# Attention's page stores on ACT's queue, the third group of the next stage in raw tiles, residual rows tied to the splits

## The chip, the cores and the metric

The kernel runs on one core of a Trainium2 chip. The time is device microseconds (us) of one execution, the median of several runs. TensorE is called PE here, VectorE DVE, ScalarE ACT, GpSimd POOL and SyncE SP.

## What is computed

A two-layer encoder trunk on 1024 positions of width 1024 in float32. Each layer is a mixer and a SwiGLU block, each followed by a LayerNorm over the scaled residual. Layer 0's mixer is latent attention with 8 heads beside a 2-D Fourier mix; layer 1's is a spatial gating unit. Cut to what matters here:

```python
def even_mixer(x, ...):
    attn = mla_attention(q_nope, q_rope, k_nope, k_rope, v)      # 8 heads, softmax over 1024 keys
    return jnp.concatenate([attn, fourier_mix(f)], axis=-1) @ w_out

def reference(x, ...):
    for layer in range(DEPTH):                                   # DEPTH = 2, DN_ALPHA = 4 ** 0.25
        y = even_mixer(x, ...) if layer % 2 == 0 else odd_mixer(x, ...)
        x = layer_norm(DN_ALPHA * x + y, mix_ln_g[layer], mix_ln_b[layer])
        x = layer_norm(DN_ALPHA * x + swiglu(x, ...), ffn_ln_g[layer], ffn_ln_b[layer])
    return x
```

## The kernel before

Float32 products are made of three float32r matmuls (`mm3`, L141 to L143): each operand is split into a high part, cast by ACT (L135), and a low part, a subtraction on DVE (L136). In the trace the high part of a left operand is `xoh`, the low part `xol`; a pair is ready when its L136 has run.

The order is: `even_front` (0 to 175 us), `attention` (to 557.5 us), and then four times a long product of a finished matrix with a weight, in `reduce` (L409): `mix` (the attention's and Fourier's pages by `w_out`), `ffn0`, `odd` and `ffn1`; between them stand `ffn` and `spatial`, which make the pages of the next product. A page is a 128x1024 tile of the left matrix in HBM (512 KB).

`reduce` works with seven products instead of eight per 2x2 block, in the order p = 1, 5, 6, 4, 7, 2, 3. For each p it goes over n groups g of page pairs (two pairs each; n is 3 in `mix`, 6 in `ffn0` and `ffn1`, 4 in `odd`), and a full group is 24 matmuls 128x512 in four PSUM banks, one per slot s. The text writes (p, g) for a group. `stream` (L387 to L398) loads the two operands of a group with SP's DMAs (L396), four of 256 KB in a full group, into tiles `rx` (six of them) and splits them. Of p = 1 the first groups are loaded early by `lead`, during the stage before, into the `raw` tiles that weights use. What p = 1 takes is a plain half of a page; p = 5, 6, 7, 3 and 4 also need sums of two pages, `SA` and `SB`, which DVE makes (`page_sums`, L317 to L320) and POOL stores (`job`, L341, from pages loaded back by L335, or `direct`, L348 and L349); `TA` and `TB` are the same for the weights. The last group of a `reduce` is made from the pages that the stage before finishes last: `mixSA_5` and `mixSB_5` (the job `last`, opened at (1, 1), its sums run behind (5, 0)), `ffn0SA_10`, `oddSA_7` and so on.

The residual rows are eight tiles `xt` of 512 KB, four per half. POOL's queue loads them (`residual`, L463): half 0 at (1, 1), half 1 at (5, 0). In all stages but `mix` two DVE passes apply the last LayerNorm's gain and offset (`gained`, L469 and L470), and `add` (L457) adds a finished bank to them. A tile of `xt` has had another use before; its load waits for the stores out of that earlier tile to land.

DVE, ACT, POOL and SP each run their instructions in the order in which the program's scheduler put them; a waiting instruction holds up all that stands behind it on its engine. `behind(mark)` keeps what is built under it behind that instruction in the order, and `self.marks` are SP's last load, the cast and the subtraction of the last `stream`. In attention each half block ends with a copy of 128x256 from PSUM (L1349, ACT) and a store of it into its page (L1351, SP), 32 in all.

## Time and profile before

| | us |
|---|---|
| median of 3 runs | 2541.53 |
| lowest and highest | 2537.37, 2542.77 |
| the profiled execution | 2541.83 |
| its span, first to last instruction | 2540.0 |
| PE busy in it | 2456.4 |
| DVE, ACT, POOL busy | 1808.9, 1111.1, 318.5 |

The mean granted clock of PE was 0.984 of full speed. In the windows below a row gives for a stretch its length, then for each engine its busy time and the number of instructions, the clock that PE was granted, the busy share of the 16 DMA engines (which reads a little over 1 when they are full) and the rate. In a timeline a row is: start, length, engine, line, operation, output tile and inputs, and in brackets the idle time of the engine just before it with what ended that.

### The profile page before, as it was taken

What the parts mean: (1) busy time and instruction counts of PE and PEld (TensorE: products, weight loads), DVE (VectorE), ACT (ScalarE), POOL (GpSimd) and SP (SyncE); (2) the same over time, 40 slices, a digit from 0 to 9 for tenths busy, and PEclk for the clock granted to TensorE, in tenths of its full rate; (3) what the DMA queues carried; (4) which work ended last, traced back from release to release, by engine and by line L of the source; (5) the groups of instructions that cost most, each with busy time, mean ns of one, the idle gap of its engine ahead of it and who ended that gap; (6) DMA issues with size and microseconds to landing.
All of it is one profiled execution on the core that took longest, in us unless ns stands there. A gap on an engine that the chain in (4) does not pass through costs nothing.

```text
span 2540.0 us, 33155 instructions
## 1 busy us (share of the span) xinstructions
PE 2456.4 (97%) x12294; PEld 2073.4 (82%) x12294; DVE 1808.9 (71%) x2537; ACT 1111.1 (44%) x1711; POOL 318.5 (13%) x527
## 2 busy tenths in 40 slices
PE   8989999998999999999999999988989999999997
PEld 6778888887878888887889998877878888887885
DVE  4348878767886776768678776768777676677667
ACT  3235555544553333333456446653463333333331
POOL 1000111010111111110002132430011111111001
PEclk9999999998999999999999999999999999999998
DMA  4122333138334444467654554667624444549553
GB/s 175 43 89 71 130 110 125 57 138 282 138 118 174 169 168 162 168 252 251 226 182 172 202 203 137 195 244 276 224 73 163 177 166 155 177 164 329 190 188 140
DMA packets 164329, 431.95 MB, mean 170 GB/s; under 512 B 20136, under 2 KB 26952, under 8 KB 164168
## 3 DMA queue, kind: packets, MB, share of 16 engines
q1 hardware_dynamic: 108216, 232.11, 27.8%
q0 software_dynamic: 55952, 197.73, 20.9%
q8 instruction: 96, 1.57, 0.2%
q14 instruction: 65, 0.53, 0.1%
HBM read 286.64 MB, written 138.41 MB: 167 GB/s over the span
## 4 chain that ended last, share of the span: by engine, by line
PE 81%; DVE 6%; issue 5%; DMA 4%; ACT 2%; POOL 1%; SPq 1%; DVEq 0%; ACTq 0%; POOLq 0%
PE b L142 18%; PE b L141 18%; PE b L143 18%; PE S L1316 6%; PE b L912 5%; PE mm L141 4%; PE mm L142 4%; PE mm L143 4%; PE mm L1335 2%; DVE xol L136 1%; DMA rx<-h 1%; PE b L848 1%; DMA x<-xs 1%; ACT xoh L135 1%; DVE st L475 1%
## 5 line engine op out<-in xcount | busy, mean ns | idle before, releaser
L135 ACT CAST whi<-raw 128x1024 fp32r<-128x1024 f32 (+3 forms) x277 | 261.2, 951 | 383.4 <-PE b L142 240.2
L135 ACT CAST xoh<-rx 128x1024 fp32r<-128x1024 f32 (+1 forms) x252 | 244.5, 1011 | 413.5 <-PE b L142 308.8
L141 PE MATMUL b<-xoh,whi 128*128 128x512 f32 x1040 | 410.7, 396 | 7.9 <-ACT xoh L135 7.9
L136 DVE TENSOR_TENSOR wlo<-raw,whi 128x1024 fp32r<-128x1024 f32 (+3 forms) x277 | 303.4, 1099 | 159.3 <-ACT whi L135 157.1
L142 PE MATMUL b<-xol,whi 128*128 128x512 f32 x1040 | 406.8, 391 | 0.0
L143 PE MATMUL b<-xoh,wlo 128*128 128x512 f32 x1040 | 406.4, 391 | 0.0
L136 DVE TENSOR_TENSOR xol<-rx,xoh 128x1024 fp32r<-128x1024 f32 (+1 forms) x252 | 287.6, 1168 | 166.0 <-ACT xoh L135 160.3
L142 PE MATMUL b<-xol,xoh 128*128 128x512 f32 x960 | 379.4, 395 | 22.3 <-DVE xol L136 22.3
L141 PE MATMUL b<-xoh 128*128 128x512 f32 x960 | 376.1, 394 | 8.5 <-ACT xoh L135 8.5
L143 PE MATMUL b<-xoh,xol 128*128 128x512 f32 x960 | 377.5, 393 | 0.0
L141 PEld LDWEIGHTS b<-xoh,whi 128*128 128x128 f32 x1040 | 196.6, 189 | 50.3 <-ACT xoh L135 8.8
L142 PEld LDWEIGHTS b<-xol,xoh 128*128 128x128 f32 x960 | 183.1, 191 | 63.3 <-DVE xol L136 25.5
L143 PEld LDWEIGHTS b<-xoh,wlo 128*128 128x128 f32 x1040 | 196.3, 189 | 41.3
L142 PEld LDWEIGHTS b<-xol,whi 128*128 128x128 f32 x1040 | 196.5, 189 | 40.4 <-issue 0.5
L141 PEld LDWEIGHTS b<-xoh 128*128 128x128 f32 x960 | 182.9, 190 | 47.6 <-ACT xoh L135 9.3
L143 PEld LDWEIGHTS b<-xoh,xol 128*128 128x128 f32 x960 | 183.1, 191 | 38.2
L663 ACT COPY y<-b 128x512 f32<-128x512 f32 x200 | 116.6, 585 | 192.7 <-PE b L143 186.1
L141 PE MATMUL b<-xah,whi 128*128 128x512 f32 x416 | 162.5, 391 | 1.3 <-ACT xah L135 1.3
L142 PE MATMUL b<-xal,whi 128*128 128x512 f32 x416 | 162.0, 389 | 0.0
L143 PE MATMUL b<-xah,wlo 128*128 128x512 f32 x416 | 161.9, 389 | 0.0
L131 DVE TENSOR_TENSOR raw<-raw,raw 128x512 f32<-128x512 f32 (+1 forms) x174 | 128.5, 739 | 28.2 <-DMA raw<-w_up 24.7
L708 DVE TENSOR_TENSOR y<-b,y 128x512 f32<-128x512 f32 x84 | 58.0, 690 | 82.9 <-PE b L143 82.6
(378 smaller groups left out, 4590.9 us busy)
## 6 DMA issues: line engine op xcount, KB each, us to landing
raw<-w_gate SPq DMA_DIRECT2D x44, 512.0 KB, 3.6
raw<-w_up SPq DMA_DIRECT2D x44, 512.0 KB
q<-w_down POOLq DMA_DIRECT2D x44, 512.0 KB, 5.3
h<-x POOLq DMA_DIRECT2D x44, 512.0 KB, 3.7
rx<-h SPq DMA_DIRECT2D x60, 256.0 KB, 3.0
rx<-w_down SPq DMA_DIRECT2D x60, 256.0 KB, 4.3
raw<-o_v SPq DMA_DIRECT2D x16, 512.0 KB, 6.1
x<-o_out POOLq DMA_DIRECT2D x16, 512.0 KB, 5.7
```

What stands on the lines that cost most here:

```text
L131: self.nc.vector.tensor_tensor(out, a, b, op=ALU.subtract)
L135: a = self.nc.scalar.copy(hi, src)
L136: return a.ins, self.nc.vector.tensor_tensor(lo, src, hi.bitcast(F32), op=ALU.subtract).ins
L141: mm(ps, lh, rh, start=start, stop=False, skip_group_check=skip)
L142: mm(ps, lh, rl, start=False, stop=False, skip_group_check=skip)
L143: mm(ps, ll, rh, start=False, stop=stop, skip_group_check=skip)
L475: nc.vector.bn_stats(stats[half, s][:, c, :], xt[half, s][:, c * 512:(c + 1) * 512])
L663: nc.scalar.copy(t, ps)
L708: self.last_v = nc.vector.tensor_tensor(sb, ps, sb, op=op).ins
L912: nc.tensor.matmul(ps[:, i * 256:(i + 1) * 256], l[:, b, k, c], r[:, k, :], start=start and k == 0 and i == 0 and m == 0, stop=k == 3 and ...
L1316: nc.tensor.matmul(sc[:, kb, :], l[:, s], r[:, kb * 512:(kb + 1) * 512], start=i == 0, stop=i == 4)
L1335: nc.tensor.transpose(ps[:, k, :], p[:, kt * P:(kt + 1) * P], self.ident)
```

## The change

The 32 page stores are issued by ACT behind the copy that fills the tile, instead of by SP. In `mix` the group (1, 2) is loaded into `raw` tiles instead of `rx`. A residual row's load is preceded by a DVE MEMSET of its first column (32 in all), placed behind the last split; the rows are asked for two at a time: half 0 at (1, 1) and (1, 2), half 1 at (1, n-1) and (5, 0). `gained` is spread one group further (half 0 up to (5, 0), half 1 from (5, 1) on), and the additions of the first product's banks stand at (5, 1) instead of at the end of p = 1.

```diff
         def load(p, g):
             if (p, g) not in ops:
-                ops[p, g] = self.stream(st, p, groups[g], raws, pairs)
+                ops[p, g] = self.stream(st, p, groups[g], self.raw_tile if st is self.stage["mix"] and (p, g) == (1, 2) else raws, pairs)
...
-        def residual(half):
-            for s in range(4):
-                nc.gpsimd.dma_start(xt[half, s], resid[token(half, s)])
+        def residual(half, s):
+
+            with self.behind(self.marks[2]):
+                nc.vector.memset(xt[half, s][:, 0:1], 0.0)
+            nc.gpsimd.dma_start(xt[half, s], resid[token(half, s)])
...
-                    residual(0)
                     last = self.job(st, M - 1, True) if st is self.stage["mix"] else None
-                if p == 5 and g == 0:
-                    residual(1)
+                if p == 1 and 0 < g < 3:
+                    for s in (2 * g - 2, 2 * g - 1):
+                        residual(0, s)
+                if (p == 1 and g == n - 1) or (p == 5 and g == 0):
+                    for s in (0, 1) if p == 1 else (2, 3):
+                        residual(1, s)
...
-                if p in (1, 5) and g > 1:
-                    spread([lambda s=s: gained(p == 5, s) for s in slots], g - 2, n - 2)
+                if p == 1 and g > 1:
+                    spread([lambda s=s: gained(0, s) for s in slots], g - 2, n - 1)
+                if p == 5 and g == 0:
+                    spread([lambda s=s: gained(0, s) for s in slots], n - 2, n - 1)
+                if p == 5 and g > 0:
+                    spread([lambda s=s: gained(1, s) for s in slots], g - 1, n - 1)
+                if (p, g) == (5, 1):
+                    for s in slots:
+                        add(0, s, lo, 1, True)
...
-                        if p == 1:
-                            add(0, s, lo, p, True)
-                        elif p == 5:
+                        if p == 5:
...
-                        else:
+                        elif p == 2:
...
                 nc.scalar.copy(page, ps)
                 o = qb % 2 * 512 + qb // 2 * 256
-                nc.sync.dma_start(mix[hp * 2 + h][:, o:o + 256], page)
+                nc.scalar.dma_start(mix[hp * 2 + h][:, o:o + 256], page)
```

What this does to the order of the engines is shown at three places. Lines behind the residual load stand two lower in the changed kernel (L469 is L471 there), and lines of the later stages ten.

First, POOL and DVE at the start of `mix`. `mix6` and `mix7` are the last two pages, loaded into `raw966` and `raw967`, from which `mixSA_5` and `mixSB_5` are made, the sums that (5, 2) needs; `x`, `q` and `y` are residual rows. POOL before:

```order
L335 DMA raw966_5668<-mix6_83 128x1024
L341 DMA mixSA_4_117<-raw878_5243 128x1024
L341 DMA mixSB_4_123<-raw879_5244 128x1024
...
L463 DMA x956_5622<-x 128x1024
L463 DMA q957_5623<-x 128x1024
L463 DMA q958_5624<-x 128x1024
L463 DMA y959_5625<-x 128x1024
L335 DMA raw967_5669<-mix7_84 128x1024
L463 DMA x952_5618<-x 128x1024
```

POOL with the change:

```order
L341 DMA mixSB_4_123<-raw879_5244 128x1024
L335 DMA raw966_5664<-mix6_83 128x1024
...
L335 DMA raw967_5665<-mix7_84 128x1024
...
L465 DMA x956_5622<-x 128x1024
L465 DMA q957_5623<-x 128x1024
...
L465 DMA x955_5621<-x 128x1024
L341 DMA mixSA_5_118<-raw966_5664 128x1024
L341 DMA mixSB_5_124<-raw967_5665 128x1024
```

The last page is now loaded ahead of all eight residual rows, and the eight stand ahead of the two stores of its sums. On DVE there, `raw964` and `raw965` are group (1, 2), `rx968` and `rx969` (5, 0), `rx974` and `rx975` (5, 1). Before:

```order
L136 TENSOR_TENSOR xol_5607<-rx969_5729,xoh_5606 128x1024
L457 SCALAR_TENSOR_TENSOR x956_5622<-x956_5622,b960_5626 128x512
L317 TENSOR_TENSOR raw967_5669<-raw966_5668,raw967_5669 128x512
L457 SCALAR_TENSOR_TENSOR q957_5623<-q957_5623,b961_5633 128x512
L318 TENSOR_TENSOR raw966_5668<-raw966_5668 128x512
L136 TENSOR_TENSOR xol_5607<-rx974_5772,xoh_5606 128x1024
L457 SCALAR_TENSOR_TENSOR q958_5624<-q958_5624,b962_5640 128x512
L457 SCALAR_TENSOR_TENSOR y959_5625<-y959_5625,b963_5647 128x512
L319 TENSOR_TENSOR raw966_5668<-raw967_5669,raw966_5668 128x512
L136 TENSOR_TENSOR xol_5607<-rx975_5777,xoh_5606 128x1024
L320 TENSOR_TENSOR raw967_5669<-raw967_5669,raw966_5668 128x512
```

With the change:

```order
L136 TENSOR_TENSOR xol_5607<-raw965_5659,xoh_5606 128x1024
L464 MEMSET x956_5622 128x1
...
L136 TENSOR_TENSOR xol_5607<-rx969_5733,xoh_5606 128x1024
L464 MEMSET x954_5620 128x1
L464 MEMSET x955_5621 128x1
L317 TENSOR_TENSOR raw967_5665<-raw966_5664,raw967_5665 128x512
L136 TENSOR_TENSOR xol_5607<-rx974_5776,xoh_5606 128x1024
L318 TENSOR_TENSOR raw966_5664<-raw966_5664 128x512
L136 TENSOR_TENSOR xol_5607<-rx975_5781,xoh_5606 128x1024
L319 TENSOR_TENSOR raw966_5664<-raw967_5665,raw966_5664 128x512
L457 SCALAR_TENSOR_TENSOR x956_5622<-x956_5622,b960_5626 128x512
L320 TENSOR_TENSOR raw967_5665<-raw967_5665,raw966_5664 128x512
```

One addition of p = 1 (L457) stands ahead of L320, where four did; MEMSETs stand ahead of the sums.

Second, DVE in `ffn0`. `rx1544` and `rx1545` are group (1, 4), `rx1546` and `rx1547` (1, 5). Before:

```order
L319 TENSOR_TENSOR x1521_9735<-x1522_9736,x1488_9550 128x512
L469 TENSOR_TENSOR q1531_9756<-q1531_9756,gb1540_9785 128x1024
L320 TENSOR_TENSOR x1522_9736<-x1520_9715,x1521_9735 128x512
L470 TENSOR_TENSOR q1531_9756<-q1531_9756,gb1541_9787 128x1024
L469 TENSOR_TENSOR x1530_9755<-x1530_9755,gb1540_9785 128x1024
L136 TENSOR_TENSOR xol_5607<-rx1544_9879,xoh_5606 128x1024
L470 TENSOR_TENSOR x1530_9755<-x1530_9755,gb1541_9787 128x1024
L136 TENSOR_TENSOR xol_5607<-rx1545_9884,xoh_5606 128x1024
L469 TENSOR_TENSOR q1532_9757<-q1532_9757,gb1540_9785 128x1024
L136 TENSOR_TENSOR xol_5607<-rx1546_9915,xoh_5606 128x1024
L470 TENSOR_TENSOR q1532_9757<-q1532_9757,gb1541_9787 128x1024
L136 TENSOR_TENSOR xol_5607<-rx1547_9920,xoh_5606 128x1024
```

With the change:

```order
L319 TENSOR_TENSOR x1521_9743<-x1522_9744,x1488_9558 128x512
L464 MEMSET x1530_9763 128x1
L136 TENSOR_TENSOR xol_5607<-rx1544_9889,xoh_5606 128x1024
L320 TENSOR_TENSOR x1522_9744<-x1520_9723,x1521_9743 128x512
L136 TENSOR_TENSOR xol_5607<-rx1545_9894,xoh_5606 128x1024
L471 TENSOR_TENSOR q1531_9764<-q1531_9764,gb1540_9793 128x1024
L472 TENSOR_TENSOR q1531_9764<-q1531_9764,gb1541_9795 128x1024
L136 TENSOR_TENSOR xol_5607<-rx1546_9925,xoh_5606 128x1024
L471 TENSOR_TENSOR x1530_9763<-x1530_9763,gb1540_9793 128x1024
L136 TENSOR_TENSOR xol_5607<-rx1547_9930,xoh_5606 128x1024
L472 TENSOR_TENSOR x1530_9763<-x1530_9763,gb1541_9795 128x1024
```

The pass over `x1530` has moved behind the splits of (1, 4) and stands now between the two of (1, 5). On POOL the load of `x1530` has moved from ahead of the stores of `ffn0SA_10` and `ffn0SB_10` to behind them.

Third, DVE in `odd`. `rx2049` and `rx2050` are group (5, 0), `rx2055` and `rx2056` (5, 1); `x2004` and `x2005` hold the last two pages, whose sums go to `oddSA_7` and `oddSB_7`. Before:

```order
L136 TENSOR_TENSOR xol_5607<-rx2049_15026,xoh_5606 128x1024
L469 TENSOR_TENSOR q2031_14829<-q2031_14829,gb2044_14910 128x1024
L470 TENSOR_TENSOR y2033_14831<-y2033_14831,gb2045_14912 128x1024
L317 TENSOR_TENSOR x2005_14624<-x2004_14623,x2005_14624 128x512
...
L470 TENSOR_TENSOR q2032_14830<-q2032_14830,gb2045_14912 128x1024
L320 TENSOR_TENSOR x2005_14624<-x2005_14624,x2004_14623 128x512
L457 SCALAR_TENSOR_TENSOR x2030_14828<-x2030_14828,b2034_14832 128x512
...
L457 SCALAR_TENSOR_TENSOR y2033_14831<-y2033_14831,b2038_14865 128x512
L136 TENSOR_TENSOR xol_5607<-rx2050_15031,xoh_5606 128x1024
L136 TENSOR_TENSOR xol_5607<-rx2055_15068,xoh_5606 128x1024
L136 TENSOR_TENSOR xol_5607<-rx2056_15073,xoh_5606 128x1024
```

With the change:

```order
L136 TENSOR_TENSOR xol_5607<-rx2049_15042,xoh_5606 128x1024
L136 TENSOR_TENSOR xol_5607<-rx2050_15047,xoh_5606 128x1024
L317 TENSOR_TENSOR x2005_14640<-x2004_14639,x2005_14640 128x512
L471 TENSOR_TENSOR q2031_14845<-q2031_14845,gb2044_14926 128x1024
...
L320 TENSOR_TENSOR x2005_14640<-x2005_14640,x2004_14639 128x512
L472 TENSOR_TENSOR q2032_14846<-q2032_14846,gb2045_14928 128x1024
L471 TENSOR_TENSOR y2033_14847<-y2033_14847,gb2044_14926 128x1024
L464 MEMSET x2028_14842 128x1
L136 TENSOR_TENSOR xol_5607<-rx2055_15088,xoh_5606 128x1024
L472 TENSOR_TENSOR y2033_14847<-y2033_14847,gb2045_14928 128x1024
L464 MEMSET x2029_14843 128x1
L136 TENSOR_TENSOR xol_5607<-rx2056_15093,xoh_5606 128x1024
```

The split of `rx2050` has moved ahead of the page sums; those of (5, 1) stand behind them, with two MEMSETs, which overwrite `x2004` and `x2005` and so wait until the two stores have landed.

## Rows read from the trace of the kernel before

**Rows 1.** The page's first part: busy time, share of the span, instructions

```profile
PE 2456.4 (97%) x12294; PEld 2073.4 (82%) x12294; DVE 1808.9 (71%) x2537; ACT 1111.1 (44%) x1711; POOL 318.5 (13%) x527
```

**Rows 2.** PE's waits: who was waited for, us in total, times, longest

```profile
PE b L142 <- DVE xol L136: 22.3, 8, 6.6
PE b L141 <- ACT xoh L135: 16.4, 4, 5.0
```

**Rows 3.** Windows: length, busy (instructions) of PE, PEld, DVE, ACT, POOL, clock, DMA share, GB/s

```profile
565.00:592.50 27.50, 23.05 (x89) 17.88 (x87) 15.38 (x17) 9.36 (x9) 3.55 (x7) 0.88 0.92 341
592.50:605.00 12.50, 7.54 (x25) 5.72 (x24) 6.41 (x8) 2.94 (x3) 0.00 (x0) 0.73 0.78 254
605.00:670.00 65.00, 65.00 (x289) 53.81 (x288) 55.48 (x76) 28.37 (x29) 5.52 (x7) 1.00 0.66 222
1140.00:1155.00 15.00, 9.33 (x33) 7.18 (x32) 12.24 (x12) 3.06 (x5) 1.59 (x3) 0.77 1.00 376
1690.00:1710.00 20.00, 11.07 (x51) 9.25 (x50) 12.19 (x16) 13.06 (x24) 3.11 (x5) 0.74 1.00 370
1725.00:1740.00 15.00, 8.45 (x31) 6.58 (x30) 13.90 (x17) 2.00 (x2) 2.14 (x4) 0.77 0.72 266
2320.00:2335.00 15.00, 9.82 (x34) 7.60 (x33) 11.63 (x11) 2.80 (x4) 1.59 (x3) 0.77 1.01 395
```

**Rows 4.** PE's timeline where mix goes on after its second stop

```profile
597.85 0.80 PE L141 MATMUL b<-xoh 128*128 128x512 f32 x1 [4.96 <-ACT xoh L135]
```

**Rows 5.** SP's timeline at the start of mix

```profile
558.54 0.88 SPq L396 DMA_DIRECT2D rx<-mix  x2
...
593.77 0.32 SPq L396 DMA_DIRECT2D rx<-mixSB  x1
```

**Rows 6.** ACT's timeline there

```profile
570.98 1.04 ACT L135 CAST xoh<-rx 128x1024 fp32r<-128x1024 f32 x1 [2.06 <-DMA rx<-w_out]
...
578.32 2.21 ACT L135 CAST xoh<-rx 128x1024 fp32r<-128x1024 f32 x2 [2.53 <-DMA rx<-mixTA]
...
596.75 2.94 ACT L135 CAST xoh<-rx 128x1024 fp32r<-128x1024 f32 x3 [8.47 <-DMA rx<-mixSB]
```

**Rows 7.** DVE's timeline there

```profile
587.01 0.69 DVE L320 TENSOR_TENSOR raw<-raw,raw 128x512 f32<-128x512 f32 x1
```

**Rows 8.** POOL's timeline there

```profile
587.99 0.54 POOL L341 DMA_DIRECT2D mixSB<-raw  x1 [1.19 <-DVE raw L320]
```

**Rows 9.** All page stores of attention (L1351): nanoseconds min/median/max

```profile
L1351 SPq DMA_DIRECT2D mix<-page x32: 319/325/430, 208.6 to 558.1; - x32
```

**Rows 10.** DVE's groups by line: the shortest operation on one column

```profile
L205 DVE TENSOR_SCALAR rs<-mv 128x1 f32<-128x1 f32 x32 | 4.7, 148 | 0.2
```

**Rows 11.** DVE's timeline in ffn0

```profile
1142.76 1.23 DVE L469 TENSOR_TENSOR x<-x,gb 128x1024 f32<-128x1024 f32 x1 [4.64 <-DMA x<-xs]
```

**Rows 12.** PE's timeline where ffn0 goes on

```profile
1147.44 0.79 PE L142 MATMUL b<-xol,xoh 128*128 128x512 f32 x1 [5.67 <-DVE xol L136]
```

**Rows 13.** POOL's timeline in ffn0

```profile
1132.68 0.53 POOL L463 DMA_DIRECT2D x<-xs  x1
...
1137.28 0.54 POOL L349 DMA_DIRECT2D ffn0SB<-x  x1 [1.65 <-DVE x L320]
...
1146.41 0.53 POOL L463 DMA_DIRECT2D x<-xs  x1 [0.75 <-DMA ffn0SB<-x]
```

**Rows 14.** DVE's timeline in odd

```profile
1726.10 0.69 DVE L317 TENSOR_TENSOR x<-x,x 128x512 f32<-128x512 f32 x1 [1.93 <-DMA tp<-x]
...
1734.30 5.77 DVE L136 TENSOR_TENSOR xol<-rx,xoh 128x1024 fp32r<-128x1024 f32 x5
```

**Rows 15.** PE's timeline where odd goes on

```profile
1735.58 0.79 PE L142 MATMUL b<-xol,xoh 128*128 128x512 f32 x1 [6.55 <-DVE xol L136]
```

**Rows 16.** POOL's timeline in odd

```profile
1730.56 0.54 POOL L861 DMA_DIRECT2D oddSA<-x  x1 [9.05 <-DVE x L319]
...
1733.70 0.53 POOL L463 DMA_DIRECT2D x<-xs  x1 [0.87 <-DMA oddSA<-x]
```

## Prediction

> **What bounds the kernel now.** I read the page's busy times first: PE is busy for 2456.4 us, 97% of the span [rows 1], so only the time in which it stops, or runs slowly after a stop, can be won; about 84 us. Then PE's waits: 22.3 us for low parts of the left operand of the long products and 16.4 us for high parts [rows 2], which is more than any other pair of lines has. Then the windows, since the sum doesn't tell where. In an undisturbed stretch, 605 to 670, a matmul takes 65/289 = 0.225 us [rows 3], so a group of 24 takes 5.4 us. What a stretch loses is its length less its matmuls by 0.225:
>
> - `mix`: 27.5 - 89 x 0.225 = 7.5 to 592.5 us, and 12.5 - 25 x 0.225 = 6.9 from there to 605; 14.4.
> - `ffn0`: 15 - 33 x 0.225 = 7.6.
> - `odd`: 20 - 51 x 0.225 = 8.5 at 1690 (the shapes are mixed there, so this is rough), and 15 - 31 x 0.225 = 8.0 at 1725.
> - `ffn1`: 15 - 34 x 0.225 = 7.4.
>
> These 46 us, all at the starts of the four `reduce`, are 1.8% of the time. Last I read the timelines there, for what ended each stop. In `mix` the second operand of (1, 2) is cast at 570.98 and a later one waits for `rx<-mixSB` until 596.75 [rows 6]. In `ffn0` DVE's L469 waits 4.64 us for a residual row [rows 11], and the splits of (1, 4) stand behind it. In `odd` the split of (5, 0)'s second operand stands behind gains, page sums and additions until 1734.30 [rows 14]. After a stop the granted clock falls (means of 0.73 to 0.88 in these stretches, 1.00 from 605 on [rows 3]), and matmuls run slower until it is back. `mix` loses 6.9 around a stop of 4.96 [rows 3, 4] and `ffn0` 7.6 around one of 5.67 [rows 3, 12], so a stop of 5 us costs 1.9 us more than itself. I take these 1.9 for every stop that is left.
>
> **Page stores to ACT.** 32 issues at 0.325 us [rows 9] come to 10.4 us of ACT's queue, each behind a copy. ACT is busy for 44% of the span [rows 1] and PE sets the pace of attention, so I cost this at nothing. If ACT's slack were gone the price would be all 10.4 us, which I leave to a rival. SP no longer holds the loads of (1, 2) behind the last store; before, they went out at 558.54 [rows 5].
>
> **`mix`, group (1, 2) in raw tiles.** Its loads can run during attention, into tiles that are free then. Nothing remains of the first stop, 7.5 us, and PE would want (5, 2) at 597.85 - 4.96 - 7.5 = 585.4 [rows 3, 4]. So the question is when (5, 2) is ready, and that hangs on L320. Before, L320 started at 587.01 [rows 7], its store went out at 587.99 [rows 8], the reload at 593.77 [rows 5], the cast began at 596.75 [rows 6] and PE at 597.85: 10.8 us. L320 now stands behind the splits of (5, 0) and (5, 1) and one addition of p = 1. Early end: only the end of p = 1 holds it, at 585.4 - 2 x 5.4 = 574.6, then one addition (0.6): L320 at 575.2, (5, 2) at 586.0. Late end: (5, 1) takes the place in SP's queue that (5, 0) had, whose second operand was cast at 578.32 [rows 6]; cast 1.1, split 1.15 (5.77/5 [rows 14]), L319 and the addition 0.6 each give L320 at 581.8 and (5, 2) at 592.6. I take 589.5, about the middle, since 1 MB less is queued ahead of the loads after 558. PE then stops for 4.1, with 1.9 for the slow restart: 6.0 of 14.4 are still lost, a **gain of 8.4** (5.3 to 13). The two stores of the sums now stand behind all eight residual loads, 4 MB, on POOL; that is the weak point of this term.
>
> The store is the longest piece of this chain: 5.8 us from 587.99 to 593.77 for 512 KB [rows 5, 8]. By the Trainium skill, "DMA: Bandwidth & Descriptors", section "Anatomy of one DMA", a transfer from POOL's queue takes 2.0 us plus its bytes at 436 GB/s, an estimate of 3.2 us here, and (5, 2) would come 2.6 us sooner. The row disagrees, with the DMA engines 0.78 to 0.92 busy [rows 3], and the sum goes by the row.
>
> **`ffn0` and `ffn1`.** The pass over `x1530` no longer stands ahead of (1, 4), so PE doesn't stop at 1147.44 - 5.67 = 1141.8 [rows 12] but wants (1, 5) 5.4 us later, at 1147.2. That pass now stands between the two splits of (1, 5), and its row is loaded behind the store of `ffn0SB_10`. This store was issued at 1137.28 and had landed at 1146.41, when POOL let the next load go [rows 13]. I let the row land then too: the pass 1.15, the split 1.15, (1, 5) at 1148.7, a stop of 1.5 and 1.9 for the restart, and 4.2 of 7.6 are gained. Bounds: the row took 10.1 us before (1132.68 to 1142.76 [rows 11, 13]); issued at 1137.8 it would land at 1147.9, and 2.7 are gained; landing three us sooner, all 7.6. I take **4** each for `ffn0` and `ffn1`, whose window reads alike [rows 3].
>
> **`odd`.** (5, 0) is ready in time: PE doesn't stop at 1735.58 - 6.55 = 1729.0 [rows 15] and runs to 1734.4. But (5, 1) now stands behind L317, which waits for a page's store until 1726.10 [rows 14], three more page sums (0.6 each) and five gains (1.15 each), until 1734.3. The MEMSET of `x2028` asks that `oddSA_7` has landed, 3.1 us after its issue (1730.56 to 1733.70 [rows 16]), which is done by then. One split, one gain and the other split bring (5, 1) to 1737.7. A stop of 3.3 and 1.9 leave 2.8 of 8.0, and some of it goes again at (5, 2), behind the four additions. I take **2** (-1 to 6). The stop at 1692 waits for other loads, and I leave its 8.5 as they are; one residual row less beside them could give back 1.4 (512 KB at 370 GB/s [rows 3]), which is in the range only.
>
> **MEMSETs.** 32 operations on one column; the trace has none, the nearest is 148 ns [rows 10], so 4.7 us of DVE in all, 1.2 per stage, beside PE. Up to 0.6 each, as a page sum takes, they would add 4 us of DVE work to a stage, of which the part ahead of a late split counts: 8 MEMSETs by 0.45, at most 3.6 a stage.
>
> **The sum.** 8.4 + 4 + 2 + 4 = 18.4, so the profiled execution's 2541.8 becomes 2523.4. It is 0.3 above the median of the runs shown: **2523 us**. A measurement of this kernel can tell about 0.2% from no change, 5.1 us.
>
> **Rivals.**
>
> *All four stops go* (0.12). The row lands early in `ffn0` and `ffn1`, L320 runs at the end of p = 1, and `odd` finds DVE free: 14.4 + 7.6 + 8.0 + 7.4 = 37, or 2504 us. For it: DVE is idle for some of the stretch in `ffn0` (12.2 of 15 us busy). Against it: in `odd` it is busy for 13.9 of 15 [rows 3].
>
> *The traffic decides, not the order* (0.20). The DMA engines are 0.92 to 1.01 busy in four of the six stretches [rows 3]. If a stop ends when the bytes ahead of it are in, whatever queue asked, only the 1 MB that leaves the crowded stretch of `mix` counts, 3.1 us at its 341 GB/s [rows 3], besides 2 in `odd`, where the share was 0.72: 2536.5 us, on the edge of what can be told. This is what the Trainium skill, "DMA: Bandwidth & Descriptors", section "Issuing engines are not separate DMA queues", would have: transfers from SP, ACT and POOL end up on the same 16 engines and interleave, and moving them between queues saves issue time only. The windows agree that these are full there; they don't show that each stop waited for the total.
>
> *A residual row becomes the stop* (0.06), slower. On DVE the pass over a row blocks the split behind it. If `x1530`, asked for 5 us later, landed 16 us after its issue instead of 10, (1, 5) would be ready at 1156.1: a stop of 8.9 plus 1.9, 3.2 more than the 7.6 of now, in `ffn0` and in `ffn1`. In `mix` the stores of the sums behind 4 MB of rows would be as late and take its gain. That is 2548 us. It decides once a row takes over 13 us. For it: the engines are full until 1155. Against it: 10.1 was the longest before.
>
> *The raw tiles come free late, or ACT loses time* (0.04). The loads of (1, 2) then wait for stores out of these tiles and land near the time of before, or PE waits for ACT in attention. The gain of `mix` is gone: 2532 us.
>
> **How the numbers follow.** The forecast has 0.58. The first two rivals hold the ends: the range is 2508 to 2537, short of the first one's 2504 and up to the second's 2536.5. Faster by over 0.2%, below 2536.4, are the forecast, the first and the last rival and half of the second, 0.84; within 0.2% the other half, 0.10; slower 0.06.
>
> **What would show it.** In the profile after, the stop near 568 must be gone, and a cast of a `raw` tile for (1, 2) must stand before 557; L320 should start between 575 and 582 after which PE stops for 1 to 7 us. L471 must no longer stand ahead of (1, 4), and PE's stops in `ffn0` and `ffn1` should fall from over 5 us to under 3. In `odd` the stop should sit before (5, 1) instead of (5, 0). PE busy should change little and attention keep its length. The prediction is wrong if a stop of 5 us is still there in `ffn0`, if MEMSETs or L471 show waits of more than 4 us ahead of a split, or if `mix` waits for its sums as late as 597.

## The result and the profile after

The changed kernel takes 2524.18 us against 2539.69 for the kernel before in the same runs, a ratio of 0.9935 (95% interval 0.9918 to 0.9952): 0.65% faster. The prediction was 2523.0. In a second set of runs it took 2522.22 against 2538.94, 0.9934 (0.9920 to 0.9947). The first profile of the changed kernel was of a disturbed execution, so all rows of it here are from the second set, called e_again below.

The page's first part, with the columns of [rows 1]; the span is 2519.2 us where it was 2540.0:

```profile
PE 2451.5 (97%) x12294; PEld 2069.8 (82%) x12294; DVE 1809.1 (72%) x2569; ACT 1112.0 (44%) x1711; POOL 318.9 (13%) x527
```

The work is the same, but for 32 more instructions on DVE. PE is busy for 4.9 us less with the same matmuls, and its mean granted clock is 0.989 where it was 0.984; the other 15.9 of the 20.8 us are idle time, most of them in PE's waits (who was waited for, total, times, longest; [rows 2] has those of before):

```profile
PE b L141 <- ACT xoh L135: 14.8, 3, 6.9
PE b L142 <- DVE xol L136: 14.6, 8, 4.2
...
PE b L858 <- ACT whi L849: 5.0, 1, 5.0
```

22.3 us of waits for low parts have become 14.6, and 16.4 for high parts 14.8. The third row is the first stop of `odd`; before, it was 8.93 us.

PE's timeline of the changed kernel at the five places where the long products stop:

```profile
589.67 0.80 PE L141 MATMUL b<-xoh 128*128 128x512 f32 x1 [6.90 <-ACT xoh L135]
...
1140.29 0.50 PE L142 MATMUL b<-xol,xoh 128*128 128x512 f32 x1 [1.92 <-DVE xol L136]
...
1720.09 0.50 PE L142 MATMUL b<-xol,xoh 128*128 128x512 f32 x1 [3.51 <-DVE xol L136]
...
1743.16 0.79 PE L142 MATMUL b<-xol,xoh 128*128 128x512 f32 x1 [4.16 <-DVE xol L136]
...
2315.64 0.50 PE L142 MATMUL b<-xol,xoh 128*128 128x512 f32 x1 [0.77 <-DVE xol L136]
```

In `mix` only the stop before (5, 2) is left [rows 4], at 6.90 us longer than the 4.96 of before, but PE is through it 8.2 us earlier (589.67, not 597.85); 2.3 of these this execution had won before `mix` begins. In `ffn0` 5.67 [rows 12] has become 1.92. In `ffn1` 0.77 is left, and 0.86 at 2324.96, where before had

```profile
2328.05 0.79 PE L142 MATMUL b<-xol,xoh 128*128 128x512 f32 x1 [5.18 <-DVE xol L136]
```

In `odd` 6.55 [rows 15] has become 3.51, one group later, and there is a new stop of 4.16 just ahead of p = 6.

The windows (columns as in [rows 3]) show the same for whole stretches:

```profile
565.00:592.50 27.50, 20.60 (x86) 16.67 (x85) 13.69 (x16) 6.74 (x7) 3.74 (x7) 0.86 0.92 354
592.50:605.00 12.50, 12.50 (x51) 10.20 (x50) 8.94 (x12) 4.07 (x5) 0.00 (x0) 0.90 0.89 309
...
1730.00:1745.00 15.00, 10.84 (x44) 8.62 (x43) 15.00 (x18) 4.00 (x4) 0.00 (x0) 0.90 0.37 119
```

From 592.5 to 605 PE is never idle (12.5 of 12.5, with 51 matmuls where there were 25). In the last row DVE is: 15.00 of 15.00, which is what the new stop of `odd` waits for.

To compare kernels by stage I matched matmuls of the same number in two traces and took by how many us the later kernel is ahead of before, at the start of each stage and behind its stops: at 565 and 640 us of before's trace for `mix`, 1120 and 1200 for `ffn0`, 1680 and 1800 for `odd`, 2310 and 2400 for `ffn1`. The table has what the lead grew by between the two. Medians and ratios are of the timed runs. The four stages are from one profiled execution each; stretches in which two kernels do the same differ too, all that stands ahead of `mix` by up to 4 us, so a stage is good to 1 or 2 us. What the four columns leave out of a whole span is in such stretches: for the changed kernel 2.3 us ahead of `mix`, 2.3 between the stages and 2.1 behind 2400, of 20.8.

| kernel | median us | ratio to before, 95% | mix | ffn0 | odd | ffn1 |
|---|---|---|---|---|---|---|
| predicted | 2523.0 | | 8.4 | 4 | 2 | 4 |
| e_again, the change | 2522.22 | 0.9934 (0.9920 to 0.9947) | 5.3 | 4.0 | -0.4 | 5.3 |
| e_stores | 2534.43 | 0.9981 (0.9972 to 0.9990) | 5.0 | -0.9 | -0.6 | 0.5 |
| e_mix | 2530.69 | 0.9966 (0.9953 to 0.9979) | 6.2 | 0.2 | 0.1 | 0.8 |
| e_rows | 2525.69 | 0.9950 (0.9937 to 0.9962) | 2.5 | 5.4 | -1.9 | 4.3 |
| e_order | 2531.06 | 0.9967 (0.9956 to 0.9979) | 0.6 | 5.0 | -2.2 | 5.1 |
| e_resid | 2522.60 | 0.9933 (0.9921 to 0.9945) | 3.0 | 6.0 | -0.7 | 6.4 |
| e_noorder | 2518.95 | 0.9926 (0.9914 to 0.9938) | 6.7 | 5.9 | 0.9 | 5.7 |
| e_nomemset | 2527.44 | 0.9954 (0.9942 to 0.9966) | 6.6 | 3.3 | -0.7 | 5.7 |
| e_sums_act | 2519.18 | 0.9927 (0.9914 to 0.9940) | 7.6 | 5.4 | -0.2 | 4.9 |
| e_late | 2521.03 | 0.9931 (0.9919 to 0.9944) | 7.2 | 4.9 | -1.4 | 4.9 |
| e_halves | 2517.57 | 0.9919 (0.9905 to 0.9932) | 6.5 | 6.6 | 2.2 | 6.7 |
| e_best | 2512.81 | 0.9901 (0.9885 to 0.9918) | 7.2 | 6.4 | 3.6 | 6.6 |

### The profile page after: what moved, and what is told of

Its sections match the earlier page's. It is cut to its first block, busy times and chain, and to the rows that moved or that the text cites. A ratio compares the mean times of both kernels' runs of the same rounds, so it can differ in the third digit from the quotient of the medians.

```text
span 2729.4 us, 33158 instructions
## 1 busy us (share of the span) xinstructions
PE 2680.0 (98%) x12294; PEld 2135.9 (78%) x12294; DVE 1818.6 (67%) x2569; ACT 1118.1 (41%) x1711; POOL 316.0 (12%) x527
## 4 chain that ended last, share of the span: by engine, by line
PE 94%; DMA 2%; DVE 2%; issue 1%; ACT 0%; SPq 0%; POOL 0%; DVEq 0%; ACTq 0%; POOLq 0%
PE b L141 22%; PE b L143 22%; PE b L142 22%; PE b L922 6%; PE S L1326 6%; PE mm L141 4%; PE mm L142 4%; PE mm L143 4%; PE mm L1345 2%; PE b L858 1%; DMA mixSB<-raw 0%; PE b L376 0%; DVE xol L136 0%; PE b L364 0%; DMA rx<-o_out 0%
## 5 line engine op out<-in xcount | busy, mean ns | idle before, releaser
L141 PE MATMUL b<-xoh,whi 128*128 128x512 f32 x1040 | 439.0, 422 | 7.9 <-ACT xoh L135 7.7
L143 PE MATMUL b<-xoh,wlo 128*128 128x512 f32 x1040 | 434.4, 418 | 0.0
L142 PE MATMUL b<-xol,whi 128*128 128x512 f32 x1040 | 434.0, 417 | 0.0
L142 PE MATMUL b<-xol,xoh 128*128 128x512 f32 x960 | 401.1, 418 | 4.1 <-DVE xol L136 4.0
L141 PE MATMUL b<-xoh 128*128 128x512 f32 x960 | 399.0, 419 | 4.4 <-ACT xoh L135 4.4
L143 PE MATMUL b<-xoh,xol 128*128 128x512 f32 x960 | 401.5, 418 | 0.0
L141 PE MATMUL b<-xah,whi 128*128 128x512 f32 x416 | 173.7, 419 | 0.0
L143 PE MATMUL b<-xah,wlo 128*128 128x512 f32 x416 | 173.4, 417 | 0.0
L142 PE MATMUL b<-xal,whi 128*128 128x512 f32 x416 | 173.2, 416 | 0.0
```

The source lines that it names most:

```text
L141: mm(ps, lh, rh, start=start, stop=False, skip_group_check=skip)
L142: mm(ps, lh, rl, start=False, stop=False, skip_group_check=skip)
L143: mm(ps, ll, rh, start=False, stop=stop, skip_group_check=skip)
```

## The experiments

The theory to test: four separate edits, each of which shortens the stops of its own stage, so that their gains add. The rival that had most for it: the traffic of the residual rows decides, and any edit that thins it helps.

### Again: the changed kernel itself

No edit.

> The changed kernel once more, for a profile at PE's full clock. By the prediction's sum: about 18 us below the kernel before; in the windows mix loses about 6 us instead of 14.4 (565 to 605), ffn0 and ffn1 about 3.5 instead of 7.5 each, odd's second stretch 6 instead of 8. By the rival that the traffic decides: about 5 us below, with stops of over 5 us still there in ffn0 and ffn1.

Measured: 2522.22 us, 0.9934. The size holds, the parts only in `ffn0` and `ffn1`. By the windows above `mix` still loses 27.5 - 86 x 0.225 = 8.2 and 12.5 - 51 x 0.225 = 1.0, together 9.2 us where 6 was expected, and in `odd` the stops behind 1700 add up to 7.67 us (3.51 and 4.16) where before had one of 6.55.

### Stores: the page stores alone

The kernel before, with one line of the change:

```diff
-                nc.sync.dma_start(mix[hp * 2 + h][:, o:o + 256], page)
+                nc.scalar.dma_start(mix[hp * 2 + h][:, o:o + 256], page)
```

> Only the page stores on ACT. If SP's queue was held by the last page store alone, the loads of (1, 2) go out earlier here as far as their rx tiles are free; by my sum the tiles are not, so no difference (within 2 us) from the kernel before. If ACT's slack in attention were gone: up to 10 us slower.

A miss: 2534.43 us, 4.5 below before where nothing was expected. SP's timeline, before and in this run, gives the reason. Before:

```profile
553.35 5.10 SPq L1351 DMA_DIRECT2D mix<-page  x2
558.54 0.88 SPq L396 DMA_DIRECT2D rx<-mix  x2
559.52 0.90 SPq L396 DMA_DIRECT2D rx<-w_out  x2
```

With the stores on ACT (the loads of `mix` are out since 526):

```profile
556.76 0.81 SPq L396 DMA_DIRECT2D rx<-w_out  x2
557.62 0.93 SPq L396 DMA_DIRECT2D rx<-mixSB  x2
```

Half of (1, 2), its pages of `mix`, had stood behind page stores that it doesn't depend on. Without them it goes out 32 us earlier, still into `rx` tiles, and its other half is cast at 562.28 instead of 570.98 [rows 6]. PE's first stop of before, at (1, 2),

```profile
572.08 0.79 PE L141 MATMUL b<-xoh 128*128 128x512 f32 x1 [3.53 <-ACT xoh L135]
573.34 0.80 PE L142 MATMUL b<-xol,xoh 128*128 128x512 f32 x1 [0.47 <-DVE xol L136]
```

is gone: PE passes the same two matmuls without a wait, at 567.47 and after. What is left ahead of (5, 2) are waits of 0.27 and 0.75 at (5, 1), where before waited 0.46. So the raw tiles are not needed to take this stop away.

### Mix: page stores and raw tiles

The two edits that touch `mix` alone, on the kernel before: the line above and

```diff
-                ops[p, g] = self.stream(st, p, groups[g], raws, pairs)
+                ops[p, g] = self.stream(st, p, groups[g], self.raw_tile if st is self.stage["mix"] and (p, g) == (1, 2) else raws, pairs)
```

> Only the page stores on ACT and the group (1, 2) in raw tiles; residual rows, gains and additions as before. If the first stop of mix is a matter of the loads of (1, 2) alone, it goes here too (7.5 us), but the page sums stay behind four additions, so the second stop may keep its date: 3 to 9 us below the kernel before, and ffn0, odd and ffn1 lose what they lost before. If the traffic decides, about 3 us below.

Measured: 2530.69 us, 8.2 below before; in `mix` 6.2 where 8.4 was predicted. The raw tiles are loaded during attention and cast at 558.24, and the first stop is gone. The stop before (5, 2) is 5.81 us at 590.45. `ffn0` and `odd` stop as before (5.19 and 6.38).

### Rows: all the rest of the change

The changed kernel with those two edits undone:

```diff
-                ops[p, g] = self.stream(st, p, groups[g], self.raw_tile if st is self.stage["mix"] and (p, g) == (1, 2) else raws, pairs)
+                ops[p, g] = self.stream(st, p, groups[g], raws, pairs)
...
-                nc.scalar.dma_start(mix[hp * 2 + h][:, o:o + 256], page)
+                nc.sync.dma_start(mix[hp * 2 + h][:, o:o + 256], page)
```

> Only the residual rows, gains and additions; page stores on SP and the group (1, 2) in rx tiles as before. By my sum 10 us below the kernel before (4 + 2 + 4), with the first stop of mix unchanged. If the parts add up, e_mix and e_rows together give what the whole change gives. If the traffic decides: about 2 us below.

Measured: 2525.69 us, 13.2 below before where 10 was expected, and the first stop of `mix`, expected to stay, is gone. With the 8.2 of the other half that would be 21.4, and the whole change gave 16.7: the parts overlap, and they do so in `mix`, which gained 2.5 here with neither of the edits meant for it (6.2 with these two, 5.3 with all). The run on the residual rows, below, shows how.

### Order: only the new places of gains and additions

The kernel before with the last two hunks on `gained` and `add` of the change; residual rows, page stores and (1, 2) as before:

```diff
-                if p in (1, 5) and g > 1:
-                    spread([lambda s=s: gained(p == 5, s) for s in slots], g - 2, n - 2)
+                if p == 1 and g > 1:
+                    spread([lambda s=s: gained(0, s) for s in slots], g - 2, n - 1)
+                if p == 5 and g == 0:
+                    spread([lambda s=s: gained(0, s) for s in slots], n - 2, n - 1)
+                if p == 5 and g > 0:
+                    spread([lambda s=s: gained(1, s) for s in slots], g - 1, n - 1)
+                if (p, g) == (5, 1):
+                    for s in slots:
+                        add(0, s, lo, 1, True)
```

> Only the places of gained and of the additions of p = 1; the residual rows loaded four at a time and without MEMSETs, page stores and group (1, 2) as before. Theory, in ffn0 and ffn1 it was the pass over a late row standing ahead of the splits of (1, 4): it goes behind them here too, and the row is loaded as early as before, so these stages win as much as in the changed kernel or more (4 to 7 each), odd 0 to 3, mix 0 to 2: 10 to 17 us below the kernel before. Rival, the spreading of the loads is what helps: under 5 us below.

Measured: 2531.06 us, 8.5 below before, between the 10 to 17 of the theory and the rival's 5; 5.0 in `ffn0` and 5.1 in `ffn1`: no load was moved, only DVE's order, and the stops there fell from 5.67 to 2.46 and from 5.18 to 2.09. That speaks against traffic alone. In `mix` both stops are there (3.45 and 4.70). In `odd`, where 0 to 3 was to be gained, it loses 2.2, by this new stop of PE:

```profile
1753.98 0.79 PE L142 MATMUL b<-xol,xoh 128*128 128x512 f32 x1 [4.24 <-DVE xol L136]
```

### Resid: only the residual rows' new loads

The kernel before with the rows asked for two at a time behind a MEMSET:

```diff
+            with self.behind(self.marks[2]):
+                nc.vector.memset(xt[half, s][:, 0:1], 0.0)
             nc.gpsimd.dma_start(xt[half, s], resid[token(half, s)])
...
+                if p == 1 and 0 < g < 3:
+                    for s in (2 * g - 2, 2 * g - 1):
+                        residual(0, s)
+                if (p == 1 and g == n - 1) or (p == 5 and g == 0):
+                    for s in (0, 1) if p == 1 else (2, 3):
+                        residual(1, s)
```

> Only the residual rows' loads and MEMSETs; gained and the additions where they were before. Theory: the pass over the late row still stands ahead of the splits of (1, 4) and the row comes later, so ffn0 and ffn1 lose as much as before or more, up to 5 us each, and odd gains at most 2 from fewer loads beside its first stop: from 2 us below to 8 us above the kernel before. Rival, the spreading of the loads is what helps: 6 to 12 us below.

The largest miss: 2522.60 us, 0.9933, which is the gain of the whole change. POOL's timeline at the start of `mix` in this run, where before had issued the first at 548.81, three more from 557.83 and the other four from 563.25:

```profile
566.53 0.53 POOL L465 DMA_DIRECT2D x<-x  x1 [4.73 <-DVE x L464]
567.06 1.05 POOL L465 DMA_DIRECT2D q<-x  x2
...
580.71 0.54 POOL L341 DMA_DIRECT2D mixSB<-raw  x1 [1.80 <-DVE raw L320]
```

and ACT's:

```profile
563.90 1.05 ACT L135 CAST xoh<-rx 128x1024 fp32r<-128x1024 f32 x1 [1.46 <-DMA rx<-w_out]
```

SP sends the loads of (1, 2) no earlier than before (at 556.9 and 557.9, behind the page stores), but they now run without 4 MB of rows beside them, and the second operand is cast at 563.90 instead of 570.98 [rows 6]. So the first stop of `mix` needed both, late loads and rows beside them, and either edit ends it. In `ffn0` and `ffn1` the stops are 1.58 and 0.90. On DVE's timeline in `ffn0` the pass over `x1530` stands where it no longer delays (1, 4), although `gained` has its old place in the text: the scheduler had moved it behind the first split of (1, 5), presumably because its row comes later.

```profile
1141.06 1.22 DVE L471 TENSOR_TENSOR x<-x,gb 128x1024 f32<-128x1024 f32 x1 [2.63 <-DMA x<-xs]
```

### No order: the change without the new places

The changed kernel with the hunks of the run on the order undone:

```diff
-                if p == 1 and g > 1:
-                    spread([lambda s=s: gained(0, s) for s in slots], g - 2, n - 1)
...
+                if p in (1, 5) and g > 1:
+                    spread([lambda s=s: gained(p == 5, s) for s in slots], g - 2, n - 2)
```

> The change without its last part: page stores on ACT, group (1, 2) in raw tiles, residual rows tied to the splits, but gained and the additions of p = 1 where they were before. Tying the rows alone gave 17 us, the new places of the gains alone 8 us, both together without the edits to mix 13. Theory, the parts cover for one another and the new places of the gains cost something once the rows are tied: ffn0 and ffn1 lose 1 to 2 us less than in the changed kernel, the stop before p = 6 in odd (4.16 us) is gone and the one before (5, 1) is back at 6 to 8, mix as in the changed kernel or 1 to 3 us longer for the additions ahead of L320: 0 to 4 us below the changed kernel. Rival, the parts add up: 2 to 8 us above it.

Measured: 2518.95 us, 0.9926 (0.9914 to 0.9938), 3.3 below e_again and so inside the first theory's 0 to 4; the intervals overlap. Once the rows are tied, the new places add nothing that can be told, and may cost something. In `odd` they trade one stop for two. Here it is one of 7.77 us, before (5, 0), and none ahead of p = 6 (the MEMSETs that the row names run at 1720.07, when the first split of that group, begun at 1718.91, is through):

```profile
1720.17 0.79 PE L142 MATMUL b<-xol,xoh 128*128 128x512 f32 x1 [7.77 <-DVE x L464]
```

### No MEMSET: the rows in their new places, not tied

```diff
-            with self.behind(self.marks[2]):
-                nc.vector.memset(xt[half, s][:, 0:1], 0.0)
```

> The changed kernel without the 32 MEMSETs: a residual row's load then waits only for its tile, not for a split. Theory, the MEMSETs are what holds 4 MB of rows back behind the loads of the operands: without them the rows go out early, mix's (5, 0) and (5, 1) and the last groups of p = 1 in ffn0 and ffn1 get their operands later, and 3 to 10 us of the gain are lost. Rival, the MEMSETs only cost DVE's queue some waits: the time stays within 2 us or falls.

Measured: 2527.44 us, 0.9954 (0.9942 to 0.9966), 5.2 above e_again by medians. That is as expected, but the profile doesn't bear out the reason: by stage it gains as much as the changed kernel (6.6, 3.3, -0.7, 5.7 in the table, 14.9 together against 14.2), the stops are 6.07 in `mix` and 2.61 in `ffn0`, and of the 3.5 us between the two spans (2522.7 and 2519.2) 3.1 had been lost ahead of `mix`, where the two kernels do the same. The profiled execution is also 3.0 faster than this kernel's median, so that part of the 5.2 may not be in it. What the MEMSETs are worth beside the new places of the loads stays open; the intervals of the two ratios just overlap.

### Sums on ACT: the last two stores of `mix` from another queue

```diff
-        def finish(mark):
+        def finish(mark, queue=nc.gpsimd):
...
-                nc.gpsimd.dma_start(st[d][m], r)
+                queue.dma_start(st[d][m], r)
...
-                    last(self.marks[2])
+                    last(self.marks[2], nc.scalar)
```

> The changed kernel with one edit: the two stores of the last page sums of mix (mixSA_5, mixSB_5) are issued from ACT's queue instead of POOL's, where they stand behind eight residual loads. In the changed kernel mixSB_5's store took from 572.06 to 585.95 us until SP could load it back, 13.9 us, and PE stopped for 6.90 us at (5, 2). Theory, the queue: on ACT's queue the store lands in 3 to 6 us, the stop goes, and the time falls by 7 to 9 us below the changed kernel (to about 2514). Rival, the traffic: the DMA engines are full until 580 whatever queue asks, the store still takes 11 to 14 us and the time stays within 2 us.

This and the next run ask what holds (5, 2) of `mix`. In the changed kernel DVE's last sum, POOL's store, SP's reload and ACT's cast stand at (one timeline for each engine):

```profile
571.08 0.68 DVE L320 TENSOR_TENSOR raw<-raw,raw 128x512 f32<-128x512 f32 x1
...
566.88 1.57 POOL L465 DMA_DIRECT2D x<-x  x3 [3.29 <-DMA gT<-ln_gT]
570.86 0.54 POOL L341 DMA_DIRECT2D mixSA<-raw  x1 [2.42 <-DMA q<-x]
572.06 0.54 POOL L341 DMA_DIRECT2D mixSB<-raw  x1 [0.66 <-DVE raw L320]
...
585.95 0.32 SPq L396 DMA_DIRECT2D rx<-mixSB  x1
...
588.57 2.94 ACT L135 CAST xoh<-rx 128x1024 fp32r<-128x1024 f32 x3 [9.65 <-DMA rx<-mixSB]
```

From the store to the reload it is 13.9 us, where before it was 5.8 [rows 5, 8]. The landings in this trace tell why: POOL's eight rows land at 568.7, 570.7, 572.6, 574.5, 576.4, 578.3, 580.2 and 582.1, and the two sums at 584.0 and 585.9, in the order of their issue and one about every 1.9 us. The store takes the last place in this line. The experiment's timelines (ACT's and SP's):

```profile
572.89 0.33 ACTq L341 DMA_DIRECT2D mixSB<-raw  x1
...
582.34 0.32 SPq L396 DMA_DIRECT2D rx<-mixSB  x1
...
587.42 4.84 ACT L135 CAST xoh<-rx 128x1024 fp32r<-128x1024 f32 x5 [13.03 <-DMA rx<-mixSB]
```

9.45 us with the same eight rows in flight, 4.4 less; the cast follows after 5.1 instead of 2.6, which gives over half of it back, and PE's stop is 4.46 instead of 6.90. The time is 2519.18 us, 3.0 below e_again: between the two theories, and within the overlap of the intervals.

### Late: half of `mix`'s rows asked for later

```diff
-                if (p == 1 and g == n - 1) or (p == 5 and g == 0):
+                if st is self.stage["mix"]:
+                    if (p, g) == (5, 1):
+                        for s in slots:
+                            residual(1, s)
+                elif (p == 1 and g == n - 1) or (p == 5 and g == 0):
```

> The changed kernel with one edit: in mix the four residual rows of the second half are asked for at (5, 1) instead of at (1, 2) and (5, 0), so that on POOL the stores of mixSA_5 and mixSB_5 stand behind four residual loads (2 MB) instead of eight. From ACT's queue the store still took 9.4 us until SP could load it back (13.9 in the changed kernel), so part of the delay was the queue and part the full DMA engines. Theory, both matter: with 2 MB less ahead of it in either sense the store lands in 4 to 8 us, PE's stop at (5, 2) falls from 6.90 us to under 2, and the time by 5 to 8 us below the changed kernel. Rival, only the length of the chain of store, reload and cast matters: the stop stays over 4 us and the time within 3 us.

The store of `mixSB_5` stands ahead of the last four rows here. On SP's timeline the reload follows after 8.2 us (574.03 to 582.20), and the cast only 6.0 us later, at 588.18:

```profile
582.20 0.32 SPq L396 DMA_DIRECT2D rx<-mixSB  x1
```

PE's stop is 4.36, the time 2521.03 us: 1.2 below e_again, not to be told from it, as the rival had it. The four rows that were taken out of the store's way are in the reload's: they land at 584.0 to 589.6.

### Halves: the gains in half rows

`gained` works on half a row, the halves that the next additions need first; the rest goes behind p = 6.

```diff
-                    spread([lambda s=s: gained(1, s) for s in slots], g - 1, n - 1)
+                    spread([lambda s=s, h=h: gained(h, s, hi) for s in slots for h in range(2)], g - 1, n - 1)
+                if p == 6:
+                    spread([lambda s=s: gained(1, s, lo) for s in slots], g, n)
```

> The changed kernel with gain and offset applied to half rows: the half that p = 1 adds to first, the other half beside p = 5 for both halves of the rows, and the low half of the second four during p = 6. That takes 4 x 1.15 us of DVE work out of the stretch before (5, 3) ends. Theory, DVE is the bound in odd: the stops of 3.51 us before (5, 1) and 4.16 us before the first group of p = 6 shrink to under 2 each, 3 to 6 us below the changed kernel; ffn0 and ffn1 win up to 1 us each. Rival, the loads decide: no difference beyond 2 us, since no load moves.

Measured: 2517.57 us, 0.9919 (0.9905 to 0.9932), 4.7 below e_again, inside the 3 to 6 expected, though the intervals overlap. DVE's pieces ahead of the late splits are shorter: the stop in `ffn0` is 0.92, in `ffn1` 0.58; in `odd` the one before (5, 1) is gone, and 1.63 stands before (5, 2). The stop ahead of p = 6 is unchanged, 4.24; the end of this section comes back to it.

### All three: halves, late rows and sums on ACT

The three diffs above in one kernel.

> The changed kernel with three edits together: the gains cast by half rows with the low half of the second four during the sixth group of the stream, the second half's residual rows of mix asked for at (5,1), and the last two stores of mix's and ffn's sums issued by ACT. Theory of separate places (the halves save in odd and in ffn1, the other two at the second stop of mix): 4.7 from the halves and about 3 from the other two, about 2514.5 us where the changed kernel has 2522.2, with a stop before (5,2) of mix under 4 us. Rival (the stop before (5,2) is set by the traffic of the residual rows wherever they are asked for and whoever stores): the stop stays at 4 to 5 us and the time at 2516.5 to 2518, that of the halves alone.

Measured: 2512.81 us, 0.9901 (0.9885 to 0.9918), below the interval of the changed kernel (0.9920 to 0.9947): the fastest of all. The time is the first theory's and better, but the stop is the rival's:

```profile
588.49 0.80 PE L141 MATMUL b<-xoh 128*128 128x512 f32 x1 [4.40 <-ACT xoh L135]
```

Late rows and ACT's queue together leave as much of it as either alone (4.36, 4.46), and counted from the first matmul of `mix` all three come to (5, 2) at the same time: after 31.9 us with ACT's queue, 31.8 with late rows and 31.8 here, against 34.5 in the changed kernel. The windows say what is left to hold it, in this kernel:

```profile
560.00:572.00 12.00, 12.00 (x55) 9.93 (x54) 7.19 (x12) 3.79 (x4) 4.75 (x9) 1.00 0.98 351
572.00:585.00 13.00, 12.09 (x54) 9.68 (x52) 4.76 (x11) 1.05 (x1) 2.11 (x4) 1.00 1.04 409
```

The DMA engines are full from 560 on; what (5, 2) waits for is part of 351 to 409 GB/s, whoever asks. No run takes the rows out of this stretch, so that their traffic holds what is left is argued, not shown. Where the last 4.8 us below the halves alone come from is not settled: of the 4.4 us between the two profiled spans 0.7 stand in `mix` and 1.4 in `odd`, which the two added edits don't touch, 1.0 ahead of `mix` and most of the rest between the stages, and the intervals overlap.

The new stop of `odd` stands in every kernel that has the new places of gains and additions (4.16 in the changed kernel, and 4.22, 4.24, 4.28, 4.13, 4.74, 4.24, 4.25 in e_rows, e_order, e_nomemset, e_sums_act, e_late, e_halves and e_best), and in none that hasn't (e_stores, e_mix, e_resid, e_noorder). DVE's timeline of the changed kernel shows what it waits for:

```profile
1731.43 2.35 DVE L471 TENSOR_TENSOR x<-x,gb 128x1024 f32<-128x1024 f32 x2
1733.70 2.35 DVE L472 TENSOR_TENSOR x<-x,gb 128x1024 f32<-128x1024 f32 x2
1735.98 1.27 DVE L457 SCALAR_TENSOR_TENSOR x<-x,b 128x512 f32<-128x512 f32 x2
...
1740.16 0.67 DVE L457 SCALAR_TENSOR_TENSOR x<-x,b 128x512 f32<-128x512 f32 x1
1740.76 4.62 DVE L136 TENSOR_TENSOR xol<-rx,xoh 128x1024 fp32r<-128x1024 f32 x4
```

Four gains and eight additions, 9.3 us without a gap, ahead of the first split of p = 6. The half rows shorten the gains; the eight additions stay, and so does the stop. In e_noorder, which has no stop here, three splits run at 1735.96 and the eight additions behind them, from 1739.47.

## Why the prediction was right, point by point

The forecast, 2523.0, stands 1.2 below the measured 2524.18 and 0.8 above the 2522.22 of the second set. The mechanism held in `ffn0` and `ffn1` and in the first stop of `mix`. That the total came so close is in part luck. The four terms, 18.4 together, came to 14.2 in the profile (5.3, 4.0, -0.4 and 5.3): `mix` and `odd` gave 5.5 less than said, and `ffn1` 1.3 more. And the kernel before took 2539.69 in the runs of the result where the forecast started from 2541.5, so that the change gained 15.5 us by medians (16.7 in the second set) where 18.5 was forecast.

**What bounds the kernel.** Right: PE's work is unchanged, and 14.2 of the 20.8 us between the profiled spans stand at the starts of the four stages. The other 6.6 lie in stretches that the change doesn't touch; 2.1 of them, behind 2400, ten of the eleven other kernels show as well, so they belong to the profiled execution of before.

**Page stores on ACT.** Their cost was right: 32 issues of 0.33 us on ACT, and attention kept its length (PE is 2.4 us ahead of before at its start and 2.3 at its end). What they free was seen too (the loads held behind the last store), but it was booked under the raw tiles, and alone they give 5.0 of the 6.2 us that they and the raw tiles gain in `mix` together.

**`mix`.** The first stop went, as said. The date of (5, 2) came out to 0.2 us, 589.67 for 589.5, but by luck: this execution enters `mix` 2.3 us earlier than before, and counted from the first matmul of `mix` PE goes on after 34.5 us, where the sum had 32.0 and before 40.4. The way there was not as said either. L320 ran at 571.08, not in 575 to 582 (4 to 11 us early, or 2 to 9 with the 2.3 taken off): the splits of (5, 0) and (5, 1) that I put ahead of it were early, and the single addition took 0.6 as said. Against that the 5.8 us from store to reload, taken over from before, became 13.9 us behind eight residual rows, the weak point that was named. So two errors of opposite sign cancelled in part, and the term that was mis-sized is the store's: 5.8 us in the sum, 13.9 measured, and 9.45 with the same rows from ACT's queue. The Trainium skill, "DMA: Bandwidth & Descriptors", section "Anatomy of one DMA", would have 3.2 us for this store, an estimate. The ten stores of the earlier sums, issued during attention, landed in 2.9 to 4.7 us in the trace of before and agree; the 13.9 behind other transfers does not. The gain came to 5.3, at the lower end of the range of 5.3 to 13, and PE's stop to 6.90 where 4.1 was said.

**`ffn0` and `ffn1`.** Right in size (4.0 and 5.3, 4 predicted) and mechanism: the pass over `x1530` waits between the splits of (1, 5), on DVE's timeline,

```profile
1137.87 1.23 DVE L471 TENSOR_TENSOR x<-x,gb 128x1024 f32<-128x1024 f32 x1 [5.47 <-DMA x<-xs]
1139.02 1.22 DVE L136 TENSOR_TENSOR xol<-rx,xoh 128x1024 fp32r<-128x1024 f32 x1
```

and PE stops for 1.92 us where 1.5 was said. The row took 9.3 us from its issue at 1128.55, 9.8 from that of the store of `ffn0SB_10` ahead of it, where the sum had 9.1. This wait of 5.47 us, like one of 5.78 in `ffn1`, is one of the signs that the prediction named for being wrong (L471 waiting more than 4 us ahead of a split). The sign was badly set: the sum itself made this pass wait for its row, and what counts is how far the split behind it delays PE. But the new places of the gains are only one way to this: tied rows with gains in the old places do as well (stops of 1.58 and 0.90).

**`odd`.** Nothing (-0.4) where 2 was said, inside the range of -1 to 6, and by other steps. The stop before (5, 1) is 3.51, 3.3 predicted. What was to go "again at (5, 2), behind the four additions" went one group later, ahead of p = 6, and took 4.16; the sum had no term of that size, and behind the first stop the stage lost 4.2 us against before. Against that the first stop, left as it was in the sum, fell from 8.93 to 5.02; the first line is of before, the second of the changed kernel:

```profile
1701.16 0.79 PE L848 MATMUL b<-q,whi 128*128 128x128 f32 x2 [8.93 <-ACT whi L839]
1683.91 0.79 PE L858 MATMUL b<-q,whi 128*128 128x128 f32 x2 [5.02 <-ACT whi L849]
```

The rows beside it (1688.03 and 1698.62 before, both ahead of its end) are now asked for at 1690.87 and 1698.36, both behind its end. That was put at 1.4 at most, from the rate of the window, and came to 3.9. In the single profiles the five kernels with untied rows show 7.0 to 8.9 there and the eight with tied rows 5.0 to 6.9; no run tried this stop by itself, so its cause is argued, not shown.

**MEMSETs.** Bounded by 148 ns; they take 59 ns each, 1.9 us in all, beside PE. That the trace of before has none was a misreading, and [rows 10] is not the shortest operation on one column. It has four of them, and they give the price:

```profile
L1057 DVE MEMSET fo<- 128x1 f32 x4 | 0.1, 59 | 0.0
```

The one that waits for a store in `odd` waits 0.19 us:

```profile
1716.36 0.06 DVE L464 MEMSET x<- 128x1 f32 x1 [0.19 <-DMA oddSA<-x]
```

**The rivals.** "All four stops go" fell: 6.90, 1.92, 3.51 and 0.77 are left. "A residual row becomes the stop" fell in `ffn0` and `ffn1`: the row took 9.3 us, below the 13 at which it decides. In `mix` its other half, the sums' stores behind 4 MB of rows, came true and took part of the gain. "The raw tiles come free late, or ACT loses time" fell: the first raw tile of (1, 2) is cast at 556.14. "The traffic decides" is half true, which the sum had no place for: in `ffn0` and `ffn1` DVE's order alone gives the gain (e_order), so traffic alone is out; but in `mix` thinning the rows alone ends the first stop (e_resid), and the second is set by the line on POOL's queue in the changed kernel and, by the windows, by full DMA engines once that is shortened. The Trainium skill, "DMA: Bandwidth & Descriptors", section "Issuing engines are not separate DMA queues", says that transfers started by the scalar, sync or gpsimd engine end up on the same 16 DMA engines and interleave, so that starting them from several engines saves only the time of the issue. Two runs speak against it as a rule for the time: page stores moved from SP to ACT gave 4.5 us, since loads that stood behind them in SP's queue went out earlier, and the sums' store from ACT's queue let the reload go 4.4 us sooner than from POOL's, behind the rows. What is left of the stop in `mix` with the store on ACT, 4.46 us, and the 4.40 of all three edits agree with it.

**Parts that add.** That the stages add was assumed; within `mix` the edits don't: e_mix and e_rows give 8.2 and 13.2, together 16.7, since either ends the first stop. The sum was spared this because it priced each stop only once.

## What to carry to other kernels

Where a stop has two causes that each need the other (a load sent late, and traffic beside it), the cheapest edit that removes either can be worth the whole, and a second edit on the same stop little: here the page stores alone gain 5.0 us in `mix` where the whole change gains 5.3, and over the whole kernel the tied residual rows alone give a ratio of 0.9933 where the change gives 0.9934. A transfer's duration in a row holds only for what was queued with it; when a change puts megabytes ahead of a store on the same queue, the store's row has to be priced anew. And work moved away from one late split lands ahead of another: look for what DVE does without a gap ahead of each later group, and cut it into pieces that the splits can pass between.

## What the runs showed of the hardware that was not expected

A 512 KB store by POOL landed after 2.9 to 13.9 us, by what was queued ahead. It was 2.9 to 4.7 for the ten stores of before that were issued during attention. Behind eight rows it was 13.9, 13.4, 13.5, 13.8 and 13.4 (e_again, e_noorder, e_halves, e_nomemset, e_rows), 9.3 where the store was issued 9.3 us after the last row instead of 4.1 to 5.5 (e_resid), and 8.2 behind four. Counted from the issue of the last row, these six reloads go out after 17.7 to 19.2 us, whenever the store was issued. From ACT's queue, with the same eight rows in flight on POOL's, the reload went 9.45 us after the store (9.77 in e_best). An engine's DMA queue thus is a place in line, beside its share of the 16 engines. That share is in the rows too: with the sums' stores on ACT's queue two of the rows on POOL's land 3.1 us after the one ahead of them instead of 1.9 (e_sums_act).

The DMA engines read full (0.96 and 1.04) at 339 and at 415 GB/s in `mix` of one kernel (e_noorder), and at 376 and 395 in the two feed-forward products before [rows 3], so their busy share doesn't tell the rate within a fifth.

A MEMSET of one column of 128 rows takes 59 ns on DVE, in both kernels; the next shortest on one column, a COPY, takes 145, and a TENSOR_SCALAR 148 [rows 10].
